# A two-layer hybrid decoder: the first weight chunk in five units between the halves of x, small inputs later and in groups

## The chip, the cores and the metric

The kernel runs on one core of a Trainium2 chip. The metric is the device time of one execution in microseconds (us), the median of three runs. The profile shows one further execution: PE is the tensor engine (PEld its weight loads), DVE the vector engine, ACT the scalar engine, POOL GpSimd, SP the engine that issues the DMAs (SPq its queue). An engine runs its instructions in the order in which they stand in its stream, so an instruction that waits holds up all behind it on that engine.

## The reference, cut to what matters

256 tokens of width 1024 pass through two layers. Each layer is

```python
h = rms_norm(x, attn_norm_g[l])
proj = h @ w_in[l]                       # 1024 x 3656, cut into 12 groups of columns
moba = moba_attention(qk(mq), qk(mk), mv)
diff = diff_attention(dq, dk, dv, lam)   # lam from diff_lambda: exp(sum) - exp(sum) + const
dsa  = dsa_attention(sq, sk, sv, iq, ik, iw)   # an indexer picks keys
x = x + concat(moba, diff, dsa) @ w_out[l]
h2 = rms_norm(x, ffn_norm_g[l])
x = x + (silu(h2 @ w_gate[l]) * (h2 @ w_up[l])) @ w_down[l]
```

qk() is a norm per head with a gain (q_norm_g, k_norm_g) and a rotary embedding.

## The kernel before, in words

**Tiles.** The 256 tokens are two tiles t of 128. The width of 1024 is 8 k-tiles of 128, and x[t] arrives in two halves hf of 512 columns, which hold k-tiles 0 to 3 and 4 to 7. Every matrix product is done in three matmuls (`mm3`, lines 442 to 444): each operand is split into a high and a low part, and high x high, low x high and high x low are added up in a PSUM bank.

**Weights.** They come as a stream of units of at most 1 MB, in the order of use. A unit's DMA (issued by SP, line 323) fills one of three `raw` tiles. ACT copies the raw tile into its high part `wh` (line 232), DVE computes the low part `wl` (line 414), in pieces of 1024 columns. Only when the last `wl` of a unit is done may SP issue the load that reuses its `raw` tile. High and low parts have four tiles.

**The first chunk.** The columns of w_in are taken in chunks: idx (456 columns), sv_iq (384), mqk, dq, dk, sqk (512 each), mv (256), dv (512). Each has a low unit (k-tiles 0 to 3) and a high one (4 to 7); mv has one unit, and the very first chunk, idx, has three here: k-tiles 0-1, 2-3 and 4-7.

**The start.** PE runs transposes of an identity (line 988) until there are operands. A half of x is transposed by four PE instructions (line 460), multiplied by the norm's gains on DVE (line 476, `w`), and split into `hH` (ACT) and `hL` (DVE, line 481). The gains come as rows (`grows`) and are turned into columns `gcol` by a PE transpose (line 1000) and a DVE copy (line 1001): those of the attention norm at the start, the rest ("late" gains) when their two loads are there.

**Small inputs.** `load_small` (lines 971 to 977) issues seven loads on SP in one go, before the fourth weight unit: rope tables, q and k gains (`gqk`), causal penalties (`pens`), the late gains in two loads, and `diff_lambda`, which DVE reduces to one number a layer (lines 1025 and 1036).

**What sets the order.** A planner (`Timeline`) interleaves threads into the five streams before the kernel is built: each request names its engine and a planned duration, and the next instruction is always the one that can start first by the planner's clocks. So planned durations and due times decide the order of the streams; semaphores between engines follow from the data.

Of the kernel before, what the change touches and what calls it, by code (L numbers as in the profile page):

```python
# [29 lines left out]
# columns of w_in, cut where the groups lie next to each other  # L30
# [20 lines left out]
class Slots:  # L51
    """Tiles handed out one at a time; each comes back with the time it is free at."""
# [118 lines left out]
def hybrid_block(  # L171
# [54 lines left out]
    def copy_op(dst, src, n, sbuf=False, scale=None, bank=None):  # L226
        """a copy (scaled, perhaps) on whichever of ACT and DVE is free first"""
# [19 lines left out]
    loaded = Event()  # the small inputs  # L247
# [12 lines left out]
    lamb = tile_([P, depth, 4, HD], tag="dqk_f4", own=False)  # L260
# [15 lines left out]
    ATT = Slots(["a", "b", "c"])  # heads with scores in PSUM at a time  # L276
# [40 lines left out]
    def load_cols(src, kts, c0, c1):  # L317
        """k-tiles kts of columns c0:c1 as [P, nk, w]."""
# [28 lines left out]
    def chunk_units(l, name):  # L347
        """the k-tiles of each of a chunk's units; small ones for the very first"""
        if l == 0 and name == "idx":
            return [[0, 1], [2, 3], hi4]  # L350
        if CHUNKS[name][1] - CHUNKS[name][0] <= 256:
            return [lo4 + hi4]
        return [lo4, hi4]

    plan = []
    for l in range(depth):
# [6 lines left out]
        for fc in range(NFC + 1):  # L363
# [3 lines left out]
            if fc > 0:  # L367
# [4 lines left out]
        key: {"n": n, "w": w, "dma": dma, "raw": Event(), "ready": Event(),  # L372
              "h": [Event() for _ in range(0, n, PIECE)]}
# [4 lines left out]
    def load_thread():  # L378
        for n, u in enumerate(units.values()):
# [27 lines left out]
    def low_thread():  # L407
        for u in units.values():
            for n, cs in enumerate(pieces(u["n"])):
# [5 lines left out]
                )  # L415
            RAW.put(raw, t)
            ahead[0] += 1
            u["ready"].done(t)
# [4 lines left out]
    def weight(*key):  # L423
# [11 lines left out]
    def mm3(o, aT, kt, tok, w, k, cols, start, stop):  # L435
        """o += a.T @ w over one k-tile, from the high and low parts of both."""
# [27 lines left out]
    def norm_thread(t, hf, g0, ready):  # L464
        """g * x of one half of the columns, transposed, in high and low parts"""
# [41 lines left out]
    def norm(g0):  # L507
        """spawns RMSNorm of both tiles; returns the events of hT's halves and of rx"""
# [10 lines left out]
    def residual_thread(t, hf, bank, done, ready, last):  # L519
        """x += a finished half of a projection back to the model's width"""  # L520
# [9 lines left out]
    def rope_apply(bank, b, nh, t, cv, sv_, dst):  # L530
        """dst[P, nh, 64] = rope(rx * b); b a PSUM view [P, nh, 64]."""
# [24 lines left out]
    def head_rstd(bank, b, n, t, dst, done):  # L556
        """1/rms over each head of rx * b into dst [P, n]"""
# [33 lines left out]
    def to_pairs(src, dsts, t, done):  # L591
        """src [P, 2n heads, 64] token-major -> the pairs of heads, dims on partitions"""
# [12 lines left out]
    def qk_thread(t, bank, full, r_ready, parts, rstd, done, r_done):  # L605
        """parts: (first head, heads, table, key?, destination) of a chunk of q and k heads"""
# [38 lines left out]
    def idx_thread(t, bank, full, r_ready, done):  # L645
        """heads 2..7 of iq, ik, iw"""
        yield ("wait", full)
        yield ("wait", r_ready)
# [41 lines left out]
    def indexer(t, ready, scored, done, rank):  # L690
        yield ("wait", ready)
        n = kspan(t)
# [289 lines left out]
    def warm_up():  # L982
# [8 lines left out]
        while not started:  # L991
            e = yield T(430.0 if e < 5000.0 else 215.0, emit)
# [344 lines left out]
```

## Time and profile before

| | |
|---|---|
| device time, median of 3 runs | 676.73 us (676.66 to 677.25) |
| span of the profiled execution, first to last instruction | 674.6 us |
| between the two | 2.1 us |
| PE busy | 665.1 us (99%) |
| DVE, ACT, POOL busy | 450.6, 356.5, 70.3 us |
| granted PE clock, mean of the span | 1.000 |

The profile gives the profiled execution's span and no further time of its own; a run's time holds some 2.1 us that lie outside the span. Busy PE time contains everything from a matmul's start to its modelled end, so neighbouring matmuls overlap: the distance between two starts is what one costs.

### The profile page before, as it was taken

Reading aid. Unit: us, or ns where it says so; the run is one execution under the profiler, and the core shown is the slowest. Engines: PE = TensorE matmul, PEld = TensorE weight load, DVE = VectorE, ACT = ScalarE, POOL = GpSimd, SP = SyncE. Lnnn points to the kernel's source line nnn. Section 1 sums busy time; section 2 is a strip of 40 time slices with the busy share of each in tenths; the row PEclk is TensorE's granted clock in tenths of the full one; section 3 lists DMA queues with packets and bytes.
Section 4 is the critical chain, followed back from the end, with each engine's and each line's share of the span. In section 5 each row is a group of like instructions: output and inputs, shape, how many; then the busy total and the mean of one; then the engine's idle time right before and its main releaser. Section 6 shows DMA issues by size and latency. Waiting matters only on the chain.

```text
span 674.6 us, 8930 instructions
## 1 busy us (share of the span) xinstructions
PE 665.1 (99%) x3264; PEld 546.2 (81%) x3264; DVE 450.6 (67%) x848; ACT 356.5 (53%) x657; POOL 70.3 (10%) x107
## 2 busy tenths in 40 slices
PE   8899999999999999999999999999999999999997
PEld 7877887888888888888888778878888888888886
DVE  5899999767655555555587999994865555555542
ACT  5564857757444444444365576686654444444430
POOL 1412240013200000000020233201000000000000
PEclk9999999999999999999999999999999999999999
DMA  8881343445655555555447215352375555555501
GB/s 259 274 297 63 106 145 119 147 144 158 234 185 188 187 184 188 186 182 177 143 158 230 84 63 180 134 157 93 127 249 187 188 187 188 188 187 188 187 1 62
DMA packets 73743, 111.28 MB, mean 165 GB/s; under 512 B 2626, under 2 KB 54628, under 8 KB 73700
## 3 DMA queue, kind: packets, MB, share of 16 engines
q1 hardware_dynamic: 73668, 110.71, 49.5%
q8 instruction: 25, 0.41, 0.2%
q14 instruction: 18, 0.15, 0.1%
q10 hardware_dynamic: 32, 0.01, 0.0%
HBM read 109.66 MB, written 1.05 MB: 164 GB/s over the span
## 4 chain that ended last, share of the span: by engine, by line
PE 95%; DMA 2%; DVE 2%; issue 0%; SPq 0%; ACT 0%; DVEq 0%
PE bank L442 28%; PE bank L444 27%; PE bank L443 27%; PE bank L460 5%; PE bank L781 3%; PE bank L706 2%; PE bank L814 2%; DMA dqk_f<-in_diff_lambda_dram 1%; DMA raw<-in_w_in_dram 1%; PE bank L816 1%; DVE wl L414 0%; DVE w L476 0%; SPq L385 0%; DVE w L1025 0%; DVE x L523 0%
## 5 line engine op out<-in xcount | busy, mean ns | idle before, releaser
L414 DVE TENSOR_TENSOR wl<-raw,wh 128x1024 fp32r<-128x1024 f32 (+1 forms) x208 | 247.1, 1209 | 55.8 <-ACT wh L232 55.7
L232 ACT ACTIVATE wh<-raw 128x1024 fp32r<-128x1024 f32 (+1 forms) x208 | 209.8, 1042 | 57.5 <-PE bank L444 51.7
L442 PE MATMUL bank<-wh,hH 128*128 128x512 f32 (+3 forms) x608 | 239.0, 393 | 0.3 <-ACT hH L232 0.3
L443 PE MATMUL bank<-wl,hH 128*128 128x512 f32 (+3 forms) x608 | 231.4, 381 | 1.5 <-DVE wl L414 1.5
L444 PE MATMUL bank<-wh,hL 128*128 128x512 f32 (+3 forms) x608 | 231.9, 381 | 0.5 <-DVE hL L481 0.5
L442 PEld LDWEIGHTS bank<-wh,hH 128*128 128x128 f32 x608 | 114.4, 188 | 24.9 <-issue 6.0
L444 PEld LDWEIGHTS bank<-wh,hL 128*128 128x128 f32 x608 | 114.2, 188 | 22.1 <-DVE hL L481 0.8
L443 PEld LDWEIGHTS bank<-wl,hH 128*128 128x128 f32 x608 | 114.5, 188 | 20.0 <-DVE wl L414 1.9
L947 ACT ACTIVATE p<-bank,rx 128x256 f32<-128x256 f32 x44 | 20.9, 475 | 111.4 <-PE bank L444 111.3
L951 DVE SCALAR_TENSOR_TENSOR p<-bank,rx,p 128x256 f32<-128x256 f32 x44 | 21.3, 484 | 77.4 <-ACT p L947 77.3
L442 PE MATMUL bank<-wh,dqk_f 128*128 128x512 f32 x176 | 71.2, 405 | 0.0
L443 PE MATMUL bank<-wl,dqk_f 128*128 128x512 f32 x176 | 69.6, 396 | 0.0
L444 PE MATMUL bank<-wh,dqk_f 128*128 128x512 f32 x176 | 69.3, 394 | 0.0
L232 ACT ACTIVATE dqk_f<-bank 128x256 fp32r<-128x256 f32 (+1 forms) x52 | 21.7, 417 | 45.1 <-PE bank L460 44.9
L963 DVE TENSOR_TENSOR dqk_f<-bank,dqk_f 128x256 fp32r<-128x256 f32 x44 | 18.5, 421 | 35.5 <-ACT dqk_f L232 35.5
L444 PEld LDWEIGHTS bank<-wh,dqk_f 128*128 128x128 f32 x176 | 33.0, 187 | 8.1
L443 PEld LDWEIGHTS bank<-wl,dqk_f 128*128 128x128 f32 x176 | 33.1, 188 | 7.1
L442 PEld LDWEIGHTS bank<-wh,dqk_f 128*128 128x128 f32 x176 | 33.0, 188 | 7.1
L766 ACT ACTIVATE p<-p,small 128x128 f32<-128x128 f32 (+1 forms) x64 | 28.4, 450 | 5.2 <-DVE small L755 5.2
L460 PEld LDWEIGHTS bank<-ident,p 128*128 128x128 f32 x160 | 21.2, 139 | 8.6 <-ACT p L766 0.3
L460 PE MATMUL bank<-ident,p 128*128 128x128 f32 x160 | 28.0, 272 | 0.0
L442 PE MATMUL bank<-wh,mH 128*128 128x512 f32 x64 | 26.6, 415 | 0.0
(108 smaller groups left out, 636.8 us busy)
## 6 DMA issues: line engine op xcount, KB each, us to landing
raw<-in_w_in_dram SPq DMA_DIRECT2D x22, 1024.0 KB, 5.0
raw<-in_w_gate_dram SPq DMA_DIRECT2D x44, 512.0 KB, 3.7
raw<-in_w_up_dram SPq DMA_DIRECT2D x44, 512.0 KB, 4.8
raw<-in_w_down_dram SPq DMA_DIRECT2D x22, 1024.0 KB, 5.0
raw<-in_w_out_dram SPq DMA_DIRECT2D x8, 1024.0 KB, 4.9
raw<-in_w_in_dram SPq DMA_DIRECT2D x4, 768.0 KB, 5.7
raw<-in_w_in_dram SPq DMA_DIRECT2D x3, 912.0 KB, 4.8
x<-in_x_dram SPq DMA_DIRECT2D x4, 256.0 KB, 3.2
```

Source lines behind the costliest of these rows:

```text
L232: nc.scalar.activation(dst, src, AF.Copy)
L414: lambda: nc.vector.tensor_sub(lo[:, cs], raw[:, cs], h[:, cs].bitcast(F32)),
L442: nc.tensor.matmul(o, aH[:, kt, tok], wH[:, k, cols], start=start, stop=False)
L443: nc.tensor.matmul(o, aH[:, kt, tok], wL[:, k, cols], start=False, stop=False)
L444: nc.tensor.matmul(o, aL[:, kt, tok], wH[:, k, cols], start=False, stop=stop)
L460: nc.tensor.transpose(o, i, ident)
L706: nc.tensor.matmul(bank[:, i * n : (i + 1) * n], iqT[rows, h // 2, toks(t)], ikT[rows, 0, :n], start=True, stop=True,)
L766: lambda: nc.scalar.activation(p[:, spans[t]], p[:, spans[t]], AF.Exp, bias=mn[:, t : t + 1], scale=-1.0, accum_out=se[t],),
L781: nc.tensor.matmul(bank[:, t * P : t * P + n], qT[rows, pair, toks(t)], kT[rows, pair, :n], start=True, stop=True,)
L947: FC, lambda: nc.scalar.activation(ff, bank[:, 0:FC], AF.Silu, scale=rx[t]), ap=1, bank=bank
L951: lambda: nc.vector.scalar_tensor_tensor(ff, bank[:, FC : 2 * FC], rx[t], ff, op0=OP.mult, op1=OP.mult),
L963: e = yield V(256, lambda: nc.vector.tensor_sub(lo, b2[:, 0:2, :], h.bitcast(F32)), bank=bank2)
```

## The change

The chunk idx is cut into five units (k-tile 0, k-tile 1, then pairs), and each of the first four stands between two halves of x. `load_small` is gone; its loads stand in four groups before later weight units (5, 6, 8, 10), and diff_lambda is loaded by its own thread, after the last group, into a `w2` tile. Threads that read a small input now wait for its group. The units of weights become ready for the planner piece by piece (`ready` is a list; `weight` takes k). The planner's cost of `mm3` rises from 3 to 13 ns a matmul above the columns, and three of its start times move. All comments are gone, and line numbers shift by one to forty.

```diff
-SMALL_FIRST = 3
+SMALL_FIRST = {5: "ropes", 6: "gqk", 8: "pens", 10: "late"}
...
-X_FIRST = {0: [(0, 0), (1, 0)], 1: [(0, 1), (1, 1)]}
+X_FIRST = {0: [(0, 0)], 1: [(1, 0)], 2: [(0, 1)], 3: [(1, 1)]}
...
         if l == 0 and name == "idx":
-            return [[0, 1], [2, 3], hi4]
+            return [[0], [1], [2, 3], [4, 5], [6, 7]]
...
-            if n == SMALL_FIRST:
-                e = yield ("op", [("DMA", 2700.0, load_small)])
-                loaded.done(e + 2000.0)
+            if n in SMALL_FIRST:
+                for ns, dma in LOADS[SMALL_FIRST[n]]:
+                    e = yield ("op", [("DMA", ns, dma)])
+                small_in[SMALL_FIRST[n]].done(e + 2000.0)
...
+                u["ready"][n].done(t)
             RAW.put(raw, t)
             ahead[0] += 1
-            u["ready"].done(t)
...
-        yield ("wait", u["ready"])
         n, w = u["n"], u["w"]
+        for ready in u["ready"][: -(-(k + 1) * w // PIECE)]:
+            yield ("wait", ready)
...
-        return T(3 * (max(n, 256) / 2.4 + 3), emit)
+        return T(3 * (max(n, 256) / 2.4 + 13), emit)
...
+    LOADS = {
+        "ropes": [(
+            600.0, lambda: nc.sync.dma_start(ropes, rope.rearrange("(t p) s d -> p t s d", p=P))
+        )],
+        "gqk": [(1600.0, load_gains)],
+        "pens": [(800.0, lambda: nc.sync.dma_start(pens, causal.rearrange("s p k -> p s k")))],
+        "late": [(800.0, load_late)],
+    }
...
-            e = yield T(430.0 if e < 5000.0 else 215.0, emit)
+            e = yield T(430.0 if e < 4800.0 else 215.0, emit)
...
         yield ("wait", start)
-        junk = yield ("get", W2)
+        w2 = yield ("get", W2)
+        lamb = w2[:, : depth * 4 * HD].rearrange("p (l f d) -> p l f d", l=depth, f=4)
+        e = yield (
+            "op",
+            [("DMA", 600.0, lambda: nc.sync.dma_start(
+                w2[:, : depth * 4 * HD],
+                diff_lambda.rearrange("l f d -> (l f d)").partition_broadcast(P),
+            ))],
+        )
...
     early = Event()
-    early.done(4500.0)
-    tl.clock["DMA"] = 2100.0
+    early.done(3400.0)
+    tl.clock["DMA"] = 900.0
```

What this does to the streams stands in the built programs. **SP, the first loads.** `x_71` and `x_72` are the two token tiles, each loaded in two halves; `raw` are weight units. Before:

```order
L385 DMA x_71<-in_x_dram 128x512
L385 DMA x_72<-in_x_dram 128x512
L323 DMA raw_90<-in_w_in_dram 128x2x456
L385 DMA x_71<-in_x_dram 128x512
L385 DMA x_72<-in_x_dram 128x512
L323 DMA raw_91<-in_w_in_dram 128x2x456
L323 DMA raw_92<-in_w_in_dram 128x4x456
L971 DMA ropes_82<-in_rope_dram 128x2x128
```

And now, from the same place:

```order
L385 DMA x_71<-in_x_dram 128x512
L322 DMA raw_89<-in_w_in_dram 128x456
L385 DMA x_72<-in_x_dram 128x512
L322 DMA raw_90<-in_w_in_dram 128x456
L385 DMA x_71<-in_x_dram 128x512
L322 DMA raw_91<-in_w_in_dram 128x2x456
L385 DMA x_72<-in_x_dram 128x512
L322 DMA raw_89<-in_w_in_dram 128x2x456
L322 DMA raw_90<-in_w_in_dram 128x2x456
L983 DMA ropes_81<-in_rope_dram 128x2x128
L322 DMA raw_91<-in_w_in_dram 128x4x384
L974 DMA gqk_82<-in_q_norm_g_dram 128x384
```

The last half of x is the seventh load instead of the fifth, and the fourth and fifth units use the raw tiles of the first and second again. The remaining small loads stand between later units: pens between the two of mqk, the late gains after the first of dq, diff_lambda after the second of sqk.

**PE, from its first instruction.** `ident` is the identity, `bank` a PSUM bank, `wh`, `wl`, `hH`, `hL` the high and low parts. Before:

```order
L988 MATMUL bank_65<-ident_73 128x128 x18
L1000 MATMUL bank_66<-ident_73,grows_78 128x16
L460 MATMUL bank_67<-ident_73,x_71 128x128 x4
L988 MATMUL bank_65<-ident_73 128x128 x2
L460 MATMUL bank_68<-ident_73,x_72 128x128 x4
L988 MATMUL bank_65<-ident_73 128x128 x16
L460 MATMUL bank_69<-ident_73,x_71 128x128 x4
L988 MATMUL bank_65<-ident_73 128x128 x2
L460 MATMUL bank_70<-ident_73,x_72 128x128 x4
L988 MATMUL bank_65<-ident_73 128x128 x4
L442 MATMUL bank_63<-wh_93,hH_147 128x456
```

Now:

```order
L996 MATMUL bank_65<-ident_73 128x128 x12
L1008 MATMUL bank_66<-ident_73,grows_78 128x16
L462 MATMUL bank_67<-ident_73,x_71 128x128 x4
L996 MATMUL bank_65<-ident_73 128x128 x6
L462 MATMUL bank_68<-ident_73,x_72 128x128 x4
L996 MATMUL bank_65<-ident_73 128x128 x8
L462 MATMUL bank_69<-ident_73,x_71 128x128 x4
L996 MATMUL bank_65<-ident_73 128x128 x4
L444 MATMUL bank_63<-wh_92,hH_146 128x456
L445 MATMUL bank_63<-wl_93,hH_146 128x456
L446 MATMUL bank_63<-wh_92,hL_147 128x456
L462 MATMUL bank_70<-ident_73,x_72 128x128 x4
```

The transposes of the last half of x stand behind the first three matmuls instead of ahead of all. The transpose of the late gains, which stood between the 24th and the 25th matmul of idx, now stands in mqk's first unit, behind nine of its matmuls.

**DVE, where diff_lambda is reduced.** It stood in the middle of the splits of idx. Now it stands behind the work on mqk's heads (`qr`) and the indexer's scores (`sco`); the last of these rows is the first of the four reductions:

```order
L728 SCALAR_TENSOR_TENSOR sco_162<-w_26_101,iw_164,sco_162 128x128
L554 TENSOR_TENSOR qr_105<-qr_105,w_25_100 128x256
L728 SCALAR_TENSOR_TENSOR sco_162<-w_26_101,iw_164,sco_162 128x128
L539 SCALAR_TENSOR_TENSOR qr_105<-bank_69,rx_166,rc_150 128x256
L728 SCALAR_TENSOR_TENSOR sco_163<-w_28_103,iw_165,pens_83 128x256
L415 TENSOR_TENSOR wl_93<-raw_89,wh_92 128x1024
L546 SCALAR_TENSOR_TENSOR w_25_100<-bank_69,rx_166,rs_151 128x4x32
L580 TENSOR_REDUCE small_122<-w_26_101 128x8
L546 SCALAR_TENSOR_TENSOR w_25_100<-bank_69,rx_166,rs_151 128x4x32
L539 SCALAR_TENSOR_TENSOR qr_106<-bank_70,rx_167,rc_150 128x256
L554 TENSOR_TENSOR qr_105<-qr_105,w_25_100 128x256
L1045 ISA w_27_102,lsum_88<-w_27_102 128x64
```

Sixteen DVE instructions stand between the split that releases the raw tile for sqk's second unit (whose load diff_lambda follows on SP) and the first reduction; the last eleven of them are the rows above.

## Rows read from the trace of the kernel before

**Rows 1.** The page's first lines: span; busy us (share), instructions of each engine.

```profile
span 674.6 us, 8930 instructions
PE 665.1 (99%) x3264; PEld 546.2 (81%) x3264; DVE 450.6 (67%) x848; ACT 356.5 (53%) x657; POOL 70.3 (10%) x107
```

**Rows 2.** Waits of PE over the whole span: us in total, times, longest.

```profile
PE bank L1000 <- DMA grows<-in_diff_subln_g_dram: 1.8, 1, 1.8
PE bank L443 <- DVE wl L414: 1.5, 1, 1.5
```

**Rows 3.** Busy us by stretch: length, PE, PEld, DVE, ACT, POOL, PE clock, DMA, GB/s.

```profile
30.00:60.00 30.00, 30.00 (x145) 23.60 (x144) 28.27 (x67) 19.41 (x30) 4.43 (x6) 1.00 0.57 195
110.00:340.00 230.00, 230.00 (x1085) 188.62 (x1085) 134.83 (x191) 116.75 (x203) 13.24 (x22) 1.00 0.53 175
```

**Rows 4.** PE in order of time, 1 to 24 us: start, duration [idle before <-releaser].

```profile
1.35 3.98 PE L988 MATMUL bank<-ident 128*128 128x128 f32 x18 [1.35 <-POOL nhalf L266]
...
6.57 1.91 PE L988 MATMUL bank<-ident 128*128 128x128 f32 x16
...
9.76 0.45 PE L442 MATMUL bank<-wh,hH 128*128 128x456 f32 x1
...
14.60 0.37 PE L444 MATMUL bank<-wh,hL 128*128 128x456 f32 x1
...
16.90 0.48 PE L442 MATMUL bank<-wh,hH 128*128 128x456 f32 x1
...
18.26 0.36 PE L442 MATMUL bank<-wh,hH 128*128 128x456 f32 x1
20.15 0.48 PE L443 MATMUL bank<-wl,hH 128*128 128x456 f32 x1 [1.53 <-DVE wl L414]
...
23.77 0.34 PE L442 MATMUL bank<-wh,hH 128*128 128x384 f32 x1
```

**Rows 5.** SP's queue in order of time: start, us of issuing.

```profile
0.72 0.85 SPq L385 DMA_DIRECT2D x<-in_x_dram  x2
...
3.08 0.94 SPq L323 DMA_DIRECT2D raw<-in_w_in_dram  x2
...
9.90 0.36 SPq L977 DMA_DIRECT2D dqk_f<-in_diff_lambda_dram  x1
```

**Rows 6.** DMA loads one by one, in order of issue: KB, us to landing.

```profile
x<-in_x_dram SPq DMA_DIRECT2D x1, 256.0 KB, 2.9
x<-in_x_dram SPq DMA_DIRECT2D x1, 256.0 KB, 3.2
raw<-in_w_in_dram SPq DMA_DIRECT2D x1, 456.0 KB, 6.8
raw<-in_w_in_dram SPq DMA_DIRECT2D x1, 912.0 KB, 9.1
dqk_f<-in_diff_lambda_dram SPq DMA_DIRECT2D x1, 256.0 KB, 8.2
raw<-in_w_in_dram SPq DMA_DIRECT2D x1, 1024.0 KB, 5.0
raw<-in_w_in_dram SPq DMA_DIRECT2D x1, 1024.0 KB, 5.7
```

**Rows 7.** DVE in order of time: a split, and the first reduction of diff_lambda.

```profile
8.36 1.11 DVE L414 TENSOR_TENSOR wl<-raw,wh 128x912 fp32r<-128x912 f32 x1 [0.16 <-ACT wh L232]
...
18.23 0.23 DVE L1025 CUSTOM_DVE_ANT_0 w<-dqk_f 128x64 f32<-128x64 f32 x1 [3.22 <-DMA dqk_f<-in_diff_lambda_dram]
```

**Rows 8.** DVE in order of time, 46 to 48 us.

```profile
46.58 0.49 DVE L537 SCALAR_TENSOR_TENSOR qr<-bank,rx,rc 128x256 f32<-128x256 f32 x1 [0.55 <-ACT w L573]
46.98 0.68 DVE L578 TENSOR_REDUCE small<-w 128x8 f32<-128x512 f32 x1
47.57 0.34 DVE L544 SCALAR_TENSOR_TENSOR w<-bank,rx,rs 128x128 f32<-128x128 f32 x1
47.83 0.34 DVE L724 SCALAR_TENSOR_TENSOR sco<-w,iw,sco 128x128 f32<-128x128 f32 x1
```

More of the change, by code (lines that the diff above doesn't have):

```diff
@@ L246, in hybrid_block @@
     tl = Timeline()
-    loaded = Event()
+    small_in = {k: Event() for k in SMALL_FIRST.values()}
     started = []
@@ L259, in hybrid_block @@
     grows2 = tile_([ngr - depth * KT, P], tag="grows2")
-    lamb = tile_([P, depth, 4, HD], tag="dqk_f4", own=False)
     gcol = tile_([P, ngr], tag="gcol")
@@ L371, in hybrid_block @@
     units = {
-        key: {"n": n, "w": w, "dma": dma, "raw": Event(), "ready": Event(),
-              "h": [Event() for _ in range(0, n, PIECE)]}
+        key: {"n": n, "w": w, "dma": dma, "raw": Event(),
+              "h": [Event() for _ in range(0, n, PIECE)],
+              "ready": [Event() for _ in range(0, n, PIECE)]}
         for key, (n, w, dma) in plan
@@ L647, in idx_thread @@
         yield ("wait", full)
+        yield ("wait", small_in["ropes"])
         yield ("wait", r_ready)
@@ L691, in indexer @@
         yield ("wait", ready)
+        yield ("wait", small_in["pens"])
         n = kspan(t)
@@ L1019, in lambda_thread @@
         yield ("wait", start)
-        junk = yield ("get", W2)
+        w2 = yield ("get", W2)
[7 more added lines that the diff above has]
+        )
+        here = Event()
+        here.done(e + 2000.0)
+        yield ("wait", here)
         for l in range(depth):
             for e in range(2):
+                pair = lamb[:, l, 2 * e, :], lamb[:, l, 2 * e + 1, :]
                 end = yield V(
@@ L1030, in lambda_thread @@
                 )
-        W2.put(junk, end)
+        W2.put(w2, end)
         yield A(4, lambda: nc.scalar.activation(lsum, lsum, AF.Exp), True)
@@ L1040, in lambda_thread, with table_thread @@
             )
-    def table_thread(l, loaded, done):
-        yield ("wait", loaded)
+        lam_ready.done(tl.clock["DVE"])
+    def table_thread(l, done):
+        yield ("wait", small_in["ropes"])
+        yield ("wait", small_in["gqk"])
         gl = gqk[:, :, l * 3 * HD : (l + 1) * 3 * HD].rearrange("p s (j d) -> p s j d", d=HD)
@@ L1079, in project @@
         for u, t in steps:
-            wt = yield from weight(l, name, u[0])
             for k, kt in enumerate(u):
+                wt = yield from weight(l, name, u[0], k=k)
                 if h_ready and kt % 4 == 0:
@@ L1093, in project, with main @@
                 spawn_post(t, bk[t], full[t])
-    def main(loaded):
+    def main():
         for l in range(depth):
             tables = Event()
-            tl.spawn(table_thread(l, loaded, tables), 2)
+            tl.spawn(table_thread(l, tables), 2)
             h_ready, r_ready = norm(l * KT)
@@ L1194, in main @@
                         key = (l, "out", OUT_ORDER[u][0])
-                        wt = yield from weight(*key)
+                        wt = yield from weight(*key, k=k)
                         yield ("wait", ev[mixed[OUT_ORDER[u][0]]])
@@ L1214, in down @@
                     key = (l, "down", fc)
-                    wt = yield from weight(*key)
                     yield ("wait", fev[fc][t])
@@ L1221, in down @@
                     for k, hf in order:
+                        wt = yield from weight(*key, k=k)
                         e = yield mm3(
@@ L1236, in main @@
                     for u in (0, 4):
-                        wt = yield from weight(l, "gu", fc, u)
                         if fc == 0:
@@ L1240, in main @@
                         for k in range(4):
+                            wt = yield from weight(l, "gu", fc, u, k=k)
                             e = yield mm3(
@@ L1270, in main @@
                         yield from down([fc - 1, fc], t)
+    lam_ready = Event()
     early = Event()
-    early.done(4500.0)
-    tl.clock["DMA"] = 2100.0
+    early.done(3400.0)
+    tl.clock["DMA"] = 900.0
     tl.clock["PE"] = 1200.0
@@ L1279, in hybrid_block @@
     nc.scalar.activation(warm, nhalf[:, 0:1], AF.Exp)
-    tl.spawn(gcol_thread(grows2, depth * KT, loaded, gains[1]), 9)
-    tl.spawn(main(loaded), 50)
+    tl.spawn(gcol_thread(grows2, depth * KT, small_in["late"], gains[1]), 9)
+    tl.spawn(main(), 50)
     tl.spawn(load_thread(), 1)
@@ L1284, in hybrid_block @@
     tl.spawn(low_thread(), split_rank)
-    tl.spawn(lambda_thread(loaded), 8)
+    tl.spawn(lambda_thread(small_in["late"]), 8)
     tl.run()
```

19 lines of the change are left out of this document (7 added, 12 removed).

## The prediction, made before the changed kernel ran

> **What bounds the kernel now.** I read the page first: PE is busy for 665.1 of the 674.6 us of the span [rows 1], and the view of busy time by stretch shows it full from 30 us on, at a granted clock of 1.00 (the upper of its two levels, 2.4 GHz) [rows 3]. So nothing behind the first 30 us can get faster by this change unless PE has less to do there, and it has not: the same matmuls stand in its stream, but for 12 transposes of the identity at the start. The view of PE's waits then says where PE stood still: for the second load of the late gains (1.8 us) and for a low part of idx (1.5) [rows 2], besides the 1.35 us until the identity is there [rows 4]. All lie in the first 21 us, so I walked that stretch in the timeline.
>
> **The start, before.** The first matmul of idx starts at 9.76 us, and the first of the next chunk at 23.77 [rows 4]. In between stand 48 matmuls. Where nothing waits, one start follows another in 0.21 us (from the 1st at 9.76 to the 24th at 14.60: 4.84 us for 23 steps), so 48 cost 10.1 us; they took 14.0. The 3.9 us more are two holes: from 14.60 to 16.90 (2.30 instead of 0.21, with the transpose of the late gains in it) and from 18.26 to 20.15 (1.89 instead of 0.21) [rows 4]. The first is the wait for the late gains, whose load stood behind all others. The second is DVE's: it sat idle for 3.22 us, until diff_lambda landed, at the first reduction at 18.23 [rows 7], with the last split of idx queued behind it. Its load was issued at 9.90 and took 8.2 us [rows 5, 6].
>
> **Term 1, the first matmul: 0.** In the new order the last half of x lands behind 4 x 256 KB of x and 228 + 228 + 456 KB of weights: 1936 KB with itself. Before, exactly as many bytes ended with the second unit of idx (4 x 256 + 2 x 456 KB), which was issued at 3.08 and landed 6.8 us later, at 9.9 [rows 5, 6]. So I put the last half of x at 9.9. PE's stream has only three matmuls ahead of its transposes; these need the first two loads alone and can run before 9; then PE waits. Four transposes cost 0.12 us each at the full clock (16 in 1.91 us [rows 4]), so the other 45 matmuls start at 10.4. Three are done by then (0.6 us), so this equals a start at 9.8, against 9.76. Splitting idx finer brings nothing here, because the last half of x, not the weights, now opens the stream. Bounds: if x lands as late as the 912 KB unit did relative to its bytes, 0.5 us worse; if the three small units let it through faster, at 9.0, then 0.9 us better.
>
> **Term 2, the two holes: -4.0.** If the 45 matmuls run without a hole they end at 10.4 + 45 x 0.21 = 19.8, against 23.77. The operands must be there. The last unit of idx ends at 4 x 256 + 1824 = 2848 KB, as the 912 KB unit did before, which landed at 12.7 (issued about 3.56, 9.1 us [rows 5, 6]). The two last units may be issued only when DVE has split the first and the second: a 912-column split takes 1.11 us [rows 7], these are half as long, and DVE comes to them at about 6 and 8 us, so their issue at some 6.5 and 8.5 lies ahead of the data in the queue (last half of x until 9.9). A split on ACT and one on DVE then make the last unit ready at about 15; PE wants it at 10.4 + 33 x 0.21 = 17.3. The tightest operand is the low part of the last half of x: on ACT its high part stands behind the last unit's split (12.7 + 1.0 + 0.6 = 14.3), on DVE behind the last unit's (15.5), and PE asks for it after 27 of the 45, at 16.1. The next chunk's first load follows with 128 KB of rope tables and 768 KB; by the 912 KB unit (2.8 us after the one ahead) that is 15.4, or five microseconds after its issue at 11, as a lone 1 MB load takes 5.0 [rows 6]: 16.0, split at 18.3, wanted at 19.8. Its second unit stands behind both gqk loads: some 23, wanted at about 24. All fit, the last ones by less than 1 us; so this term's bounds are -4.5 and -3.0.
>
> **Term 3, the late gains come back: +0.2.** Their transpose moves behind nine matmuls of mqk; the instruction itself (the hole's 0.1, and a slower first matmul) is paid there. Its two loads are small and stand behind dq's first unit, issued when sv_iq's second is split, at some 23.4; with 5.0 us for that unit [rows 6] they land at about 28.6. PE comes there after the 48 matmuls of sv_iq (19.8 + 48 x 0.21 x 384/456 = 28.3), four transposes and nine matmuls of mqk (each 0.21 x 512/456): 30.9. Bounds 0.2 and 1.2, the later by the two units' margins below 1 us.
>
> **Term 4, diff_lambda's wait moves to about 46 us: +0.5.** Its load now follows sqk's second unit on SP, and that unit is issued when DVE has finished a split of dk. A 1 MB load takes 5.0 to 5.7 us here, and diff_lambda itself added about 1.4 (it landed at 9.90 + 8.2 = 18.1; the load ahead of it, the second one of the late gains, let PE transpose them just before 16.90) [rows 4 to 6]: it lands 6.4 to 7.1 us after that split. DVE has 16 instructions to do meanwhile: one split of 1024 columns (1.11 us x 1024/912 = 1.25 [rows 7]), eight on 128 columns of 0.34 (rotary products and scores), six on 256 columns of up to 0.49 (L537 is one such) and one reduction of 0.68 [rows 8]. That is 7.6 us, less 0.08 each, since an instruction starts that much ahead of its predecessor's end (47.57 + 0.34 against 47.83 [rows 8]): 6.3. So DVE waits 0.1 to 0.8 us, with the rotary work of mqk, dk's last split and PE's transposes of those heads queued behind it. DVE is busy for 28.27 of the 30 us from 30 to 60 [rows 3], so it can't catch up quickly; but it idles there for other reasons too, as the 0.55 us in front of L537 [rows 8], which this wait can replace. Bounds 0 and 1.5 (twice the 0.8), I take 0.5.
>
> **Keeping the gain.** PE can only stay 4 us ahead if DVE does, which is all but full from 30 to 60 us [rows 3]. It gets its 3.22 us of idle time back [rows 7], and the reductions themselves (about 2 us, from 18.23 on beside one split) leave the stretch before 22 us for the one at 46; together 5 us, more than PE's gain. Behind 110 us DVE has room (134.83 of 230 us [rows 3]), and there the change moves only the order of work. That costs 0 as long as PE's neighbours stay the same: the number of places where PE goes from matmuls to the shorter score products is unchanged, so nothing is added.
>
> **Sum.** 0 - 4.0 + 0.2 + 0.5 = -3.3 us: a span of 671.3, and with the 2.1 us around it 673.4, against 676.73. A measurement of this kernel can tell about 0.2% (1.35 us) from no change.
>
> **A rule that speaks against it.** Before, two loads of 256 KB issued 0.43 us apart landed 0.8 us apart (0.72 + 2.9 and about 1.15 + 3.2 [rows 5, 6]): the fixed part of a load lies under the one ahead while the queue is full. The Trainium skill (DMA: Bandwidth & Descriptors, Anatomy of one DMA and Rules for kernel authors) gives each transfer about 2.0 us of fixed cost and asks for at least 1 MiB in one. By it, two more units would add 4.0 us and the kernel would come out at 677.4; by the rows they add nothing, and this is a rival below.
>
> **Rivals.**
> (a) *Later waits take back more*, the late gains, sv_iq's second unit and diff_lambda together 1 to 2.5 us more than I allow: 674.5 to 676. For it: three margins under 1 us on engines that run in order. Against: DVE's 5 us. 0.18.
> (b) *More gain*: the data come faster than before, because the small inputs, which were in flight with idx's last unit, now follow it; the stream opens at 9.0: 672.6, down to 671.5. 0.10.
> (c) *The smaller loads pay their fixed part in full.* A lone 256 KB load took 2.9 us and a queued one 0.8, so 2.1 us for each of two more units: 673.4 + 4.2 = 677.6. It needs an empty queue between them; SP issues every 0.43 us, against 0.7 to 0.8 us of data in each [rows 5, 6]. 0.05.
> (d) *PE's clock falls in the wait for the last half of x.* At the start 18 transposes took 3.98 us, 0.22 each, twice the later 0.12 [rows 4]. Another stretch as long at half speed costs 2.0: 675.4. Against: the holes of 1.8 and 1.5 us left the steps at 0.21. 0.03.
> (e) *Slower.* DVE's in-order wait for diff_lambda becomes the stall: every microsecond it is late beyond the 0.5 is passed on through the splits and the heads to PE. It makes the kernel slower by over 0.2% from 3.3 + 1.35 = 4.6 us of further lateness on, that is if it lands some 11.5 us after that split instead of 7. It took 8.2 us before, behind all other small loads [rows 6], which speaks against it. 6 us late gives 679.4. 0.06.
> My forecast has 0.58, with 672.4 to 674.4 as its own range.
>
> **Chances.** Faster by over 0.2% (below 675.4): forecast, (b) and two thirds of (a): 0.80. Within 0.2%: the rest of (a), (c), (d): 0.14. Slower: (e), 0.06. The range 672.0 to 675.8 leaves out (c), (e) and the ends of (a) and (b), 0.2 together.
>
> **What would show it.** In the changed profile: PE's waits hold no late gains and no wl of idx in the first 25 us, but one of 0.5 to 1.5 us for the last half of x near 9; the first 384-column matmul near 19.8; DVE idle about 1 us for diff_lambda near 45 to 47; PE full from there on. Wrong, if idx's matmuls show a new hole for a weight unit or for hL; if DVE's wait at diff_lambda exceeds 2 us and PE shows one as long behind it; or if the first matmul of sv_iq is early and the end is not, which would make DVE's backlog the bound.

## The result, and the profile after

| | before | changed |
|---|---|---|
| device time, median of 5 runs each | 676.73 us (676.58 to 677.25) | 672.33 us (671.70 to 672.52) |
| ratio | | 0.9929, 95% interval 0.9917 to 0.9941 |
| span of the profiled execution | 674.6 us | 670.2 us |

The kernel is faster by 4.4 us of span, 2.1 us again lie outside. Forecast were 673.4 us and a span 3.3 us shorter. The page's first lines, which answer to [rows 1], and the view of PE's waits, which answers to [rows 2] (us in total, times, longest):

```profile
span 670.2 us, 8938 instructions
PE 662.6 (99%) x3252; PEld 544.7 (81%) x3252; DVE 450.2 (67%) x849; ACT 359.1 (54%) x675; POOL 75.2 (11%) x107
```
```profile
PE bank L996 <- POOL nhalf L265: 1.3, 1, 1.3
PE bank L446 <- DVE hL L483: 1.0, 2, 0.5
PE bank L462 <- DVE p L955: 0.8, 2, 0.4
PE bank L462 <- DVE qr L664: 0.5, 1, 0.5
PE bank L444 <- ACT hH L232: 0.3, 1, 0.3
```

The waits for the late gains and for a low part of idx are gone; the longest wait left behind the first 1.3 us is 0.5 us. PE in order of time, against [rows 4]:

```profile
8.20 0.45 PE L444 MATMUL bank<-wh,hH 128*128 128x456 f32 x1
...
8.89 0.60 PE L462 MATMUL bank<-ident,x 128*128 128x128 f32 x4
9.25 0.45 PE L444 MATMUL bank<-wh,hH 128*128 128x456 f32 x1
...
15.60 0.37 PE L445 MATMUL bank<-wl,hH 128*128 128x456 f32 x1
16.51 0.48 PE L446 MATMUL bank<-wh,hL 128*128 128x456 f32 x1 [0.54 <-DVE hL L483]
...
19.94 0.34 PE L444 MATMUL bank<-wh,hH 128*128 128x384 f32 x1
```

The first three matmuls start from 8.20 on, the last half of x is transposed at 8.89, the stream goes on at 9.25, and the next chunk begins at 19.94, 3.83 us sooner than the 23.77 of before. One smaller hole stands at 15.60 (0.91 instead of 0.21 to the next start): the low part of the last half of x is late. DVE in order of time shows why, and further on its wait for diff_lambda, which stood at 18.23 [rows 7]:

```profile
14.75 1.11 DVE L415 TENSOR_TENSOR wl<-raw,wh 128x912 fp32r<-128x912 f32 x1 [1.74 <-ACT wh L232]
15.77 0.68 DVE L483 TENSOR_TENSOR hL<-w,hH 128x512 fp32r<-128x512 f32 x1
...
48.27 0.22 DVE L1045 CUSTOM_DVE_ANT_0 w<-w 128x64 f32<-128x64 f32 x1 [0.91 <-DMA w<-in_diff_lambda_dram]
```

`hL` stands on DVE behind the split of idx's last unit, which waits for ACT, and ACT for that unit's load.

**The rest of the span** is best read in four stretches, bounded by the first 384-column matmul and by the start of the last addition to x (one DVE instruction, L523 before and L525 now) of each stage: layer 0 to the end of its output projection, its SwiGLU, and the same for layer 1. The view of busy time by stretch, asked for the 128 head-score matmuls alone, the products of queries and keys head by head (stretch, its length, busy us of those instructions and their count; clock, DMA share, GB/s). Before:

```profile
23.77:154.77 131.00, 11.28 (x64) 1.00 0.47 155
154.77:341.77 187.00, 0.00 (x0) 1.00 0.55 182
341.77:483.74 141.97, 10.28 (x64) 1.00 0.42 141
483.74:670.79 187.05, 0.00 (x0) 1.00 0.49 160
```

Changed:

```profile
19.94:149.64 129.70, 9.91 (x64) 1.00 0.50 166
149.64:336.17 186.53, 0.00 (x0) 1.00 0.57 182
336.17:479.99 143.82, 11.82 (x64) 1.00 0.43 140
479.99:666.58 186.59, 0.00 (x0) 1.00 0.50 161
```

So the change goes on behind the start: -1.30, -0.47, +1.85 and -0.46 us. The same 64 head scores take 1.37 us less in layer 0 and 1.54 us more in layer 1, which is most of the difference there. And SwiGLU, whose matmuls are the same, is shorter. The view of one tile, dqk_f (the operand that the down projections load as weights: duration in ns, minimum, median, maximum of each group), shows where. Before:

```profile
L442 PE MATMUL bank<-wh,dqk_f x176: 393/396/481, 177.6 to 669.9; 128*128 128x512 f32 x176
L443 PE MATMUL bank<-wl,dqk_f x176: 393/396/398, 177.8 to 670.1; 128*128 128x512 f32 x176
L444 PE MATMUL bank<-wh,dqk_f x176: 388/393/400, 178.0 to 670.4; 128*128 128x512 f32 x176
```

Changed:

```profile
L444 PE MATMUL bank<-wh,dqk_f x176: 389/389/481, 173.1 to 665.7; 128*128 128x512 f32 x176
L445 PE MATMUL bank<-wl,dqk_f x176: 387/389/396, 173.3 to 665.9; 128*128 128x512 f32 x176
L446 PE MATMUL bank<-wh,dqk_f x176: 388/389/398, 173.5 to 666.2; 128*128 128x512 f32 x176
```

The medians of the three groups, 528 matmuls in all, fell by 4 to 7 ns. The prediction has nothing of this. In the built programs one thing about that tile differs: before, diff_lambda was loaded into a tile with the same tag, made early, so the tag's place began at byte 26240 of each partition, a multiple of 64. Now the tag is first used in `main` and its place is byte 219808, 32 bytes past a multiple of 64, as `wh`, `wl`, `hH` and `hL` were and are.

### The profile page after: what moved, and what is told of

Its sections match the earlier page's. It is cut to its first block, busy times and chain, and to the rows that moved or that the text cites. A ratio compares the mean times of both kernels' runs of the same rounds, so it can differ in the third digit from the quotient of the medians.

```text
span 670.2 us, 8938 instructions
## 1 busy us (share of the span) xinstructions
PE 662.6 (99%) x3252; PEld 544.7 (81%) x3252; DVE 450.2 (67%) x849; ACT 359.1 (54%) x675; POOL 75.2 (11%) x107
## 4 chain that ended last, share of the span: by engine, by line
PE 95%; DVE 2%; DMA 1%; ACT 1%; issue 0%; POOL 0%; POOLq 0%; ACTq 0%
PE bank L444 28%; PE bank L446 27%; PE bank L445 27%; PE bank L462 5%; PE bank L785 3%; PE bank L710 2%; PE bank L818 2%; DMA raw<-in_w_in_dram 1%; PE bank L820 1%; DVE wl L415 1%; DVE w L478 1%; PE bank L996 0%; ACT L951 0%; DVE hL L483 0%; ACT wh L232 0%
## 5 line engine op out<-in xcount | busy, mean ns | idle before, releaser
L415 DVE TENSOR_TENSOR wl<-raw,wh 128x1024 fp32r<-128x1024 f32 (+4 forms) x209 | 248.8, 1210 | 55.2 <-ACT wh L232 52.4
L232 ACT ACTIVATE wh<-raw 128x1024 fp32r<-128x1024 f32 (+4 forms) x208 | 211.3, 1038 | 68.0 <-PE bank L446 50.0
L505 POOL TENSOR_TENSOR ss<-ss 128x1 f32<-128x1 f32 x8 | 2.3, 290 | 236.8 <-ACT w L493 236.8
```

Source lines behind the costliest of these rows:

```text
L232: nc.scalar.activation(dst, src, AF.Copy)
L415: lambda: nc.vector.tensor_sub(lo[:, cs], raw[:, cs], h[:, cs].bitcast(F32)),
```

## The experiments

The runs e1 to e4 were made on one chip, f1 to f3 and e5 on a second, g1 to g4 on a third and h1 to h4 on a fourth, each time with the kernel before beside them; chips differ a little, so medians are compared by their ratio to before. All are built from the changed kernel unless said otherwise. The stretches are those above, in us.

| kernel | first 384 columns | layer 0 | SwiGLU | layer 1 | SwiGLU | median | ratio to before |
|---|---|---|---|---|---|---|---|
| before | 23.77 | 131.00 | 187.00 | 141.97 | 187.05 | 676.73 | |
| changed | 19.94 | 129.70 | 186.53 | 143.82 | 186.59 | 672.33 | 0.9929 |
| e1_cost3 | 20.09 | 134.66 | 185.51 | 141.96 | 185.50 | 673.72 | 0.9966 |
| e2_before_cost13 | 23.57 | 131.34 | 187.73 | 143.44 | 187.77 | 679.46 | 1.0038 |
| e3_three_units | 19.84 | 132.55 | 186.30 | 143.47 | 186.42 | 674.43 | 0.9965 |
| e4_small_together | 21.62 | 132.99 | 186.31 | 143.53 | 186.58 | 676.55 | 1.0000 |
| f1_old_place | 19.96 | 130.47 | 187.74 | 143.54 | 187.78 | 675.30 | 0.9970 |
| f2_before_new_place | 27.27 | 130.30 | 186.03 | 141.98 | 186.03 | 674.92 | 0.9970 |
| f3_gap32 | 19.77 | 130.42 | 187.48 | 143.48 | 187.49 | 674.08 | 0.9961 |
| e5_cost_by_stage | 19.96 | 131.15 | 186.03 | 141.98 | 186.03 | 670.09 | 0.9893 |
| g1_x_sooner | 20.20 | 133.39 | 185.50 | 141.98 | 186.03 | 672.54 | 0.9939 |
| g2_cost16 | 19.49 | 133.90 | 185.42 | 141.96 | 185.51 | 672.09 | 0.9932 |
| g3_all_at_0 | 19.51 | 130.83 | 186.53 | 143.74 | 186.55 | 672.83 | 0.9944 |
| g4_old_place_32 | 19.14 | 131.58 | 186.70 | 143.65 | 186.76 | 672.72 | 0.9945 |
| h1_no_lambda_wait | 19.49 | 131.01 | 186.34 | 143.50 | 186.38 | 672.45 | 0.9932 |
| h2_changed_again | 19.02 | 131.78 | 186.33 | 143.60 | 186.32 | 672.39 | 0.9929 |
| h3_by_stage_again | 19.79 | 130.68 | 186.02 | 141.95 | 186.03 | 669.95 | 0.9892 |
| h4_late_alone | 20.29 | 136.34 | 187.05 | 141.95 | 187.04 | 677.92 | 1.0013 |

The intervals are some 0.0010 to 0.0017 on either side. One thing helps in reading the table: behind layer 0's output projection PE's stream is one of only two in all these kernels. Those that plan 3 ns there share the order of before, those that plan 13 share that of the changed kernel (compared instruction by instruction in the traces). The same order and place still give SwiGLU stretches from 185.4 to 186.0 us (e1, e5, f2, g1, g2, h3; g1 has both values in one execution), so 0.5 us in such a stretch is scatter.

**The planned cost of mm3, first.** e1_cost3:

```diff
-        return T(3 * (max(n, 256) / 2.4 + 13), emit)
+        return T(3 * (max(n, 256) / 2.4 + 3), emit)
```

> Theory O (the order that the planner writes behind 30 us is worth about 1.2 us of the 4.4 gained): with the planned cost of mm3 back at 3, the first 384-column matmul stays near 19.9, and the end comes near 673.5 (between 672.9 and 674.2). Theory S (all of the gain is made in the first 25 us, the order behind it costs nothing): 672.3, within 0.5.

e2_before_cost13 is the reverse edit in the kernel before.

> The kernel before with the planned cost of mm3 at 13 and nothing else. Theory O: the start keeps its two holes (first 384-column matmul near 23.8) and the end comes 1.2 earlier, at 675.5 (674.9 to 676.2). Theory S: 676.7, within 0.5. If order effects only scatter, with no sign of their own, anything from 675 to 678.

e1 lost 1.4 us by its median and 2.5 us by the ratio (0.0037 of 676.7). Theory O's 1.2 is near the first, but its reason fails: all of the loss and more is in layer 0 (+4.96), while layer 1 (-1.86) and SwiGLU (-1.0 each) are better than in the changed kernel. And the same cost makes the kernel before 2.6 us slower, outside all that was expected: +1.47 in layer 1 and +0.7 in each SwiGLU. So behind 155 us the higher cost is a loss wherever it stands. In layer 0 the order of e1 holds head scores of 12.09 us (2.18 more) and two waits for `p` there that the changed kernel has not, 1.1 us. Counted from one start to the next in the timeline, the 36 transposes of `p` in that stretch cost 5.64 us instead of 3.31 (these two waits are in the 2.33) and the head scores 1.97 us more; together that is 4.3 of the 4.96:

```profile
20.09:154.75 134.66, 12.09 (x64) 1.00 0.48 160
```
```profile
PE bank L462 <- ACT p L770: 1.1, 2, 0.6
```
```profile
124.55 1.08 PE L462 MATMUL bank<-ident,p 128*128 128x128 f32 x6 [0.56 <-ACT p L770]
126.18 0.44 PE L462 MATMUL bank<-ident,p 128*128 128x128 f32 x2 [0.54 <-ACT p L770]
```

**The parts of the start.** e3_three_units undoes the five units (and counts the small loads' places anew, so that they stay before the same weight units):

```diff
-X_FIRST = {0: [(0, 0)], 1: [(1, 0)], 2: [(0, 1)], 3: [(1, 1)]}
+X_FIRST = {0: [(0, 0), (1, 0)], 1: [(0, 1), (1, 1)]}
-            return [[0], [1], [2, 3], [4, 5], [6, 7]]
+            return [[0, 1], [2, 3], hi4]
```

> The changed kernel with the old order of x and idx in three units; small inputs late and in groups. Theory A (the holes are closed by the small inputs alone): no wait for late gains, none for a low part of idx above 1 us, first 384-column matmul at 20 to 20.8, end at 672.3 to 673.2. Theory B (without five units the 912 KB unit comes too late for DVE to split it): a wait of 1.5 us or more at its low part, first 384-column matmul at 21.5 or later, end at 674 or more.

e4_small_together puts all small loads but diff_lambda's before weight unit 5; diff_lambda, though expected with them, follows three weight units later in the built program:

```diff
-SMALL_FIRST = {5: "ropes", 6: "gqk", 8: "pens", 10: "late"}
+SMALL_FIRST = {5: ["ropes", "gqk", "pens", "late"]}
```

> The changed kernel with all four groups of small inputs, and diff_lambda with them, loaded in one go before the first unit of the chunk behind idx. If spreading them matters: that unit lands some 3 us later than 16.9, PE waits 2 to 3 us before the first 384-column matmul (22 or later), and the end is at 674 to 675. If only their place behind idx matters and the raw tiles set the pace anyway: first 384-column matmul at 20 to 20.5, DVE's wait for diff_lambda of 0.9 us near 48 gone, end at 672.3 or up to 0.5 below.

h4_late_alone has the small loads late and in groups, and the three units, the order of x, the cost of 3 and the place of dqk_f4 as before. The other parts of the change stay in it: weights that become ready piece by piece, the planner's start times, diff_lambda's own thread.

> The order of x, the three units of idx, the cost of mm3 and the place of dqk_f4 as before; only the small inputs are late, in groups, with diff_lambda last. If the start's gain is all theirs and stays: first 384-column matmul near 19.9, end near 673 (3 to 4.5 us less than before). If the new order of layer 0 takes it back, as in the changed kernel with cost 3, where that stage took 134.7: 675 to 677.

With three units the next chunk starts at 19.84 instead of 19.94: theory A, the five units give the start nothing. But e3 as a whole is 2.4 us slower than the changed kernel by the ratio, the end that theory B gave, without B's wait: its layer 0 takes 132.55 us, with head scores of 11.56. Loaded together, the small inputs bring both old holes back in small, and with the new order of layer 0 that comes of it 4.8 us by the ratio. PE's waits of e4:

```profile
PE bank L1009 <- DMA grows<-in_ffn_norm_g_dram: 1.5, 1, 1.5
...
PE bank L446 <- DVE wl L416: 1.1, 1, 1.1
```

h4 is the sharpest: it has the start (20.29, 3.5 us sooner) and yet is no faster than before. Layer 0 takes 136.34 us, its head scores 12.73 of them against 11.28. In that profile the granted clock was also 0.50 from 130 to 133 us, so some 1.5 us of the 5.3 lost there (an estimate: half of these three) belong to that execution:

```profile
130.00:133.00 3.00, 3.00 (x11) 0.50 0.36 127
```

Another 1.1 us are waits for DVE's `qr` and `p` that before has not. So a sooner start was kept only together with another order of layer 0.

**The place of dqk_f4.** f1_old_place makes its place where it was, by an unused tile of the same tag; the five streams keep their order.

```diff
+    tile_([P, depth, 4, HD], tag="dqk_f4", own=False)
     gcol = tile_([P, ngr], tag="gcol")
```

> The changed kernel with the tile dqk_f4 (the operand that the down projections load as weights) put back to the place in SBUF where it stood before; the order of every engine stays as in the changed kernel. Theory P (the place of that tile costs PE 5 to 7 ns in each of the 528 matmuls that read it): their median goes from 389 ns back to 393 to 396, both SwiGLU stages get 1.1 to 1.4 us longer, the start stays (first 384-column matmul 19.9), and the end comes at 674.6 (674.2 to 675.2). Theory R (those matmuls are quicker because of the order or of the loads, not the place): 672.3, within 0.5.

f2_before_new_place is the kernel before with diff_lambda in a `dv` tile, which moves dqk_f4 to byte 219808.

```diff
-    lamb = tile_([P, depth, 4, HD], tag="dqk_f4", own=False)
+    lamb = dv[0].rearrange("p (l f d) -> p l f d", l=depth, f=4)
```

> The kernel before with diff_lambda loaded into a tile that is used later (dv) instead of into dqk_f4, which puts dqk_f4 to the end of SBUF; the order of PE, ACT and POOL is untouched. Theory P: the start keeps its holes (first 384-column matmul near 23.8), each SwiGLU stage goes from 187.0 to 185.5, and the end comes at 673.8 (673.3 to 674.6). Theory R: 676.7, within 0.5.

f3_gap32 and g4_old_place_32 move it by 32 bytes, with unused tiles of 32 bytes, and g3_all_at_0 moves all large tiles by 32 bytes:

```diff
+            gap = tile_([P, 8], tag="gap", own=False)          # f3
             dq_k = tile_([P, 8, S], tag="dqk_f4", own=False)
...
+    gap = tile_([P, 8], tag="gap")                             # g3
     RAW = slots(3, [P, 2048], "raw")
...
+    gap = tile_([P, 8], tag="gap")                             # g4
+    tile_([P, depth, 4, HD], tag="dqk_f4", own=False)
+    gap2 = tile_([P, 8], tag="gap2")
     gcol = tile_([P, ngr], tag="gcol")
```

> The changed kernel with an unused 32-byte tile ahead of dqk_f4, which moves it from byte 219808 to 219840 of each partition and leaves its neighbours and every order. If what counts is the tile's offset within 64 bytes (0 before, 32 in the changed kernel): the medians of the 528 matmuls go to 393 to 396 and the end to 674.6. If it is its place among the other tiles: 672.3, within 0.5.

> The changed kernel with an unused 32-byte tile ahead of all large tiles: every operand of PE, weights and moving ones, then begins at a multiple of 64 bytes, and no order changes. If a weight operand at a multiple of 64 bytes is slow by itself: all 2544 matmuls get 5 to 7 ns longer, 12 to 17 us in all, 685 to 689. If only a difference between the weight operand's and the moving operand's offset is slow: 672.3, within 0.7.

> The changed kernel with dqk_f4 in its old neighbourhood, but 32 bytes further on (byte 26272, an offset of 32 within 64 bytes, as all other operands have); no order changes. If the offset within 64 bytes makes the whole cost: medians of 389 ns, SwiGLU stages as in the changed kernel (186.6), 672.3 to 673. If the place as such costs something too: stages 0.2 to 0.3 us longer each, 672.8 to 673.5; if the offset means nothing: 675.3, as with the tile put back.

| | dqk_f4, byte | offset in 64 bytes | of wh, wl | medians, ns | the two SwiGLU |
|---|---|---|---|---|---|
| before | 26240 | 0 | 32 | 396, 396, 393 | 187.00, 187.05 |
| f1 | 26240 | 0 | 32 | 396, 396, 393 | 187.74, 187.78 |
| f3 | 219840 | 0 | 32 | 395, 395, 396 | 187.48, 187.49 |
| changed | 219808 | 32 | 32 | 389, 389, 389 | 186.53, 186.59 |
| g4 | 26272 | 32 | 32 | 394, 388, 392 | 186.70, 186.76 |
| g3 | 219840 | 0 | 0 | 389, 389, 389 | 186.53, 186.55 |
| f2 | 219808 | 32 | 32 | 389, 389, 389 | 186.03, 186.03 |

Theory P holds from both sides: putting the tile back costs 1.2 us in each SwiGLU and 0.0041 of the time (2.8 us), and moving it in the kernel before gains 1.0 in each and 2.0 us by the ratio, less than the 2.9 expected (f2's profiled execution has a hole of 2.8 us and a granted clock of 0.66 from 20 to 30 us, both ahead of these stretches). f3 shows that 32 bytes do most of it, and g3 that the offset itself is harmless: with both operands at 0 the medians are 389 again. So in these 528 matmuls a weight operand at 0 beside a moving operand at 32 is slow. g4 fits in time, less well in its medians, so a small share may belong to the neighbourhood. It is no general rule of the engine: a k-tile of idx is 1824 bytes wide, so every second one puts the moving operand at the other offset than the weights, and these matmuls of 456 columns are no slower. In g3, where they have just the pair 0 and 32, the 42 of them step at a median of 208.5 ns and the 54 with equal offsets at 208; in before (weights at 32, moving at 0) it is 206.5 against 208, 48 of each. Why 512 columns of dqk_f mind it and 456 of idx don't is open. One tile view of f3 and of g3:

```profile
L445 PE MATMUL bank<-wl,dqk_f x176: 392/395/403, 173.9 to 668.0; 128*128 128x512 f32 x176
```
```profile
L445 PE MATMUL bank<-wl,dqk_f x176: 387/389/401, 174.1 to 666.5; 128*128 128x512 f32 x176
```

**Terms 3 and 4, and the program against itself.** h1_no_lambda_wait keeps all orders and the load, but the reductions read a gain that is there:

```diff
-                pair = lamb[:, l, 2 * e, :], lamb[:, l, 2 * e + 1, :]
+                pair = gqk[:, 0, 0:HD], gqk[:, 1, 0:HD]
-                        pair[0], pair[0], pair[1], scale=1.0,
+                        junk, pair[0], pair[1], scale=0.0,
```

> The changed kernel with the four reductions of diff_lambda reading a gain that has long been loaded (lambda then is not the reference's); the load itself stays, and no order changes. If DVE's wait of 0.9 us near 48 is passed on to PE, as the term of +0.5 says: 0.4 to 0.9 us less than the changed kernel run beside it. If DVE catches up before PE needs it: no difference, within 0.3.

> The changed kernel itself, for the comparison on one chip: 672.3 to 672.8. Its trace shows how far the stages of one and the same program differ between runs: the stage up to the output projection of layer 0 within 1 us of 129.7 if its order sets it.

672.45 against 672.39: the wait of 0.9 us on DVE, which h1 has not, costs nothing. The two traces of the same program show something else. In h2 the next chunk starts 0.92 us sooner, and PE gives it back at the transposes of sv_iq's heads, where the wait for `qr` is 1.5 us instead of 0.5:

```profile
28.28 0.33 PE L462 MATMUL bank<-ident,qr 128*128 128x128 f32 x1 [1.50 <-DVE qr L664]
```

Nine traces have this order of layer 0 (changed, h1, h2, h3, e5, f1, f3, g3, g4). Their layer 0 ends between 149.64 and 151.11 us, on average at 150.47, while their starts scatter from 19.02 to 19.96, and the two with the soonest starts (h2, g4) end the stage at 150.80 and 150.72: what a start gains on 19.9 doesn't reach the end of layer 0. The 149.64 of the changed kernel's own profile is the best of the nine.

**A kernel that beats both.** e5_cost_by_stage, and h3_by_stage_again as its repeat beside the changed kernel:

```diff
+    started, pad = [], [13]
-        return T(3 * (max(n, 256) / 2.4 + 13), emit)
+        return T(3 * (max(n, 256) / 2.4 + pad[0]), emit)
...
+            pad[0] = 3
             f4s = tile_([P, 2, 4, S], F32R, tag="dqk_f4", own=False)
```

> The changed kernel with the planned cost of mm3 at 13 until the output projection of layer 0 is through, and at 3 behind it. If the stages' times belong to the orders alone and can be put together: start 19.9, layer 0 up to its output projection 129.7 as in the changed kernel, SwiGLU twice 185.5 and the mixers of layer 1 142.0 as with cost 3, so 4.0 us less than the changed kernel: 668.3 (667.7 to 669.2). If they depend on the stages ahead: 670 to 673.

> The kernel with the cost of mm3 at 13 in layer 0 and at 3 behind it, once more: 2.2 to 3.2 us less than the changed kernel beside it, if the later stages give 3.1 (1.6 in the mixers of layer 1, 0.75 in each SwiGLU); less than 1.5 if the first run was luck.

It takes 669.95 us against 672.39 on the same chip: layer 1 gives 1.65 us, each SwiGLU 0.3. The 4.0 hoped for in e5 were too many, since I had added up the best stage of each kernel: e1's SwiGLU of 185.50 and e5's of 186.03 have the same order and place, and the 129.70 of layer 0 was the best of nine. Its layer 1 holds the head scores of before, 10.28 us:

```profile
336.49:478.44 141.95, 10.28 (x64) 1.00 0.44 141
```

g1_x_sooner (`X_FIRST` ends with `2: [(0, 1), (1, 1)]`) and g2_cost16 (16 in place of 13) are built on it.

> The kernel with the cost of mm3 by stage, and the last half of x loaded one unit sooner (ahead of the 456 KB unit, behind the other half). If the hole of 0.9 us for the low part of that half near 15.3 goes: first 384-column matmul at 18.8 to 19.2 and, if layer 0 keeps its time, the end 0.8 to 1.1 earlier than the kernel with the cost by stage, 669.1. If the order of layer 0, which the planner writes anew, decides: anything from 1 us earlier to 4 later (669 to 674), with the same gain at the start.

> The kernel with the cost of mm3 by stage, with 16 in place of 13 in layer 0. PE leaves score products 11 times in layer 0 instead of 12. If these exits set that stage: 0.1 to 0.2 us less than the kernel with the cost by stage (670.0). If waits for operands between the stages' engines decide: layer 0 scatters by -1 to +4 us, 669 to 674.

Neither brings the hoped gain. g1's start isn't sooner (20.20), and both get a worse layer 0 (133.39 and 133.90); that waits and the new order decide, the second expectation of each, fits better. g2's head scores take only 10.36 us against 9.91. Its view of waits holds 1.8 us for `qr` at two places, 0.6 for `p` and 0.6 for a low part; h3 waits 1.4 for `qr`, so some 1.6 of g2's 3.2 us are waits.

## Why the prediction was right or wrong, point by point

The sign, the two holes and the start were right; the size was 1.1 us short (672.33 against 673.4, inside the range), and a good part of the gain came from what the prediction had at 0 or not at all. In spans: forecast -4.0 + 0.7 + 0 = -3.3, measured -3.83 to the first 384-column matmul, -1.30 from there to the end of layer 0's output projection, +0.92 in the three stretches behind (-0.47 + 1.85 - 0.46) and -0.2 at the end: -4.4.

- **Term 1, 0.** In this profile the last half of x came sooner than forecast: it landed at 8.67, its transposes ran at 8.89 without a wait, and the stream opened at 9.25, not 10.4. That is past the term's upper bound (9.0), and it is luck: over the nine traces of this order the stream opens between 9.25 and 10.39. In e5 and h3, where it opens at 10.37 and 10.39, the next chunk begins at 19.96 and 19.79, just as the term's sum has it. The reason that rival (b) gave, small inputs out of the way, isn't shown: in e3, which has them late too, the first 1936 KB land at 9.55 against 9.88 before. The Trainium skill (DMA: Bandwidth & Descriptors, Anatomy of one DMA) gives a transfer about 2.0 us of fixed cost; that section is on DMAs issued by GpSimd, and here SP issues them. The trace shows no such addition, since five units and three (e3) start the next chunk within 0.1 us.
- **Term 2, -4.0.** Right in sum, -3.83. The sooner opening was lost in a hole that the prediction had named as its tightest operand, `hL` of the last half of x (forecast ready after 15.5 and wanted at 16.1; it was begun at 15.77, and PE took it at 16.51). That is a new hole for `hL`, one of the prediction's own signs of being wrong; it cost 0.7 us, and six of the nine traces don't have it. That the small inputs close the holes is shown by e3 and e4; that the finer units bring the start nothing is, too.
- **Terms 3 and 4, +0.7: this sum is mis-sized.** DVE waited 0.91 us for diff_lambda, near the upper bound of 0.8, and it cost nothing (h1); the late gains caused no wait. Layer 0's stretch came out at -1.30 in the one trace and at about 0 over nine (151.47 was forecast for its end, 149.64 measured, 150.47 on average).
- **The step that failed is "Keeping the gain": behind 110 us the change moves "only the order of work", at 0.** Its premise, that nothing behind 30 us can get faster because PE is full there, took busy time for a floor; the same matmuls cost more or less by order and place. Two things of 2 to 4 us stood there with opposite signs, and that the sum came within 1.1 us is luck. The planned cost of mm3 takes, in the three stretches behind layer 0's mixers, 2.9 us in e2 against before, 2.3 in h2 against h3 and 4.0 in the changed kernel against e1. The places where PE leaves score products are as many in sum as the prediction said (13 and 13 by layer before, 12 and 14 now, counted in the built programs), but the head scores gained 1.37 us in the one layer and lost 1.54 in the other. Over all orders they tend to take longer the more often PE leaves score products: 10.36 us at 11 places (g2), 9.91 at 12, 10.28 to 11.56 at 13, 11.56 to 11.83 at 14, 11.83 at 15 (e4), 12.09 and 12.73 at 16 (e1, h4). So the prediction looked at the right thing, but only at its sum. The position of SwiGLU's transposes, which it didn't weigh, moved too, by three matmuls. The place of dqk_f4 gives 2.0 to 2.8 us back (f1, f2). Without that by-product the changed kernel would be at a ratio of 0.9970, a gain of 2.0 us.
- The other side of that step, that PE stays ahead because DVE has 5 us to spare, is not enough as a reason. h4 takes diff_lambda and the late gains out of the start in the same way and keeps nothing; the order of layer 0 differs. That the order decides is argued from e1, e3, e4 and h4, whose orders differ in several things at once.
- **Rivals.** (a) took back nothing on balance; (c), (d) and (e) did not come: no fixed cost, a granted clock of 1.000, no stall behind diff_lambda. (d) read the 0.22 us of the first 18 transposes as half the clock; the view of before has a granted clock of 1.00 from 1 to 5.4 us, so that reading isn't shown, and what made them long is open.

Still open: why an order makes layer 0 take 130 or 135 us. In e1, head scores and transposes of `p` hold 4.3 of 4.96 us, but not why they cost more. Five units with the cost of 3 and the old place, the change's start with neither by-product, wasn't run.

## What to carry to other kernels

When a change touches a planner's numbers or frees a tile, compare the later stages too, stage by stage: here the planner's order and a tile's place each moved 2 to 4 us in stages that hold no edited line. Test each part by itself before crediting it, with a kernel that only moves the tile beside it: the late small inputs with the old units, cost and place gave nothing (h4), and a place that nobody had chosen gave 2.0 to 2.8 us. Where two stages like opposite planner settings, give each its own (669.95 us).

## What the runs showed of the hardware that I had not expected

- The 528 matmuls of 128x512 that take their weights from dqk_f have medians of 393 to 396 ns where that tile is at offset 0 within 64 bytes and the moving operand at 32, instead of 389 with both at 32 (changed, f2) or both at 0 (g3); it costs 2.0 to 2.8 us of device time. In g4, with both at 32, they are 388 to 394. The 456-column matmuls of idx show nothing of the kind (medians of 206.5 to 208.5 ns from start to start at equal and at different offsets, before and g3).
- The same 64 head-score matmuls were busy for 9.91 to 12.73 us by the order of PE's stream; in every trace with the same order they take the same to 0.01 us.
- Holes in PE's start don't by themselves tell whether its clock falls. In f2's profiled execution the granted clock is 0.66 from 20 to 30 us, behind ten microseconds in which PE was busy for 7.18; the kernel before, with the same stream on PE, was busy for only 6.83 and kept 1.00. The views of busy time by stretch of f2, then of before (columns as in [rows 3], PE alone):

```profile
10.00:20.00 10.00, 7.18 (x37) 1.00 1.01 272
20.00:30.00 10.00, 9.16 (x34) 0.66 0.81 268
```
```profile
10.00:20.00 10.00, 6.83 (x33) 1.00 0.88 289
20.00:30.00 10.00, 9.63 (x51) 1.00 0.79 265
```

- On the four chips of the experiments the kernel before ran 36 of 74 times at a mean granted clock of 0.994 to 0.997, and the medians of these executions are 0.4 to 1.6 us above the others. The kernels with the changed kernel's order of layer 0 did so in none of 47 executions (the nine traces' runs). So a few tenths of a microsecond of the ratios to before come from there, and ratios from different chips are good to about 0.001.
